# A second fold of a Fourier transform over the rows, in a hybrid encoder layer

## The chip, the cores and the metric

The kernel runs on one core of one Trainium2 chip. The metric is the device time of one execution in microseconds, taken as the median of the runs. A profile of one execution gives each engine's instructions in order of time.

## The reference

Two sequences (prompt and sample) of 1024 rows and 1024 columns go through one encoder layer. Both are normalised and projected; one half of the projection feeds a latent attention with 4 heads, the other half, 512 wide in 8 groups of 64, a Fourier mixing. The results are joined, projected, added to the input, and followed by a SwiGLU feed-forward part.

```python
def fourier_group(f_in, w_four):
    b, s, _ = f_in.shape
    f = f_in.reshape(b, s, F_GROUPS, F_GROUP_DIM).astype(jnp.float32)
    fr = jnp.real(jnp.fft.fft2(f, axes=(1, 3), norm='ortho')).astype(f_in.dtype)
    out = jnp.einsum('bsgc,gcd->bsgd', fr, w_four)
    return out.reshape(b, s, FOURIER_WIDTH)

def layer(x, c, ...):
    ...
    h = rmsnorm(x, g_mix) * (1.0 + sc1) + sh1
    z = h @ w_in
    ...
    y_mla = mla_group(q_lat, kv_lat, k_pe, g_q_lat, w_uq, g_kv_lat, w_ukv)
    y_four = fourier_group(f_in, w_four)
    mix = jnp.concatenate([y_mla, y_four], axis=-1) @ w_out
    x = x + ga1 * mix
    ...
    ffn = (jax.nn.silu(h2 @ w_gate) * (h2 @ w_up)) @ w_down
    return x + ga2 * ffn
```

The real part of the 2-D transform is a cosine transform over the rows of a cosine transform over the 64 channels, less a sine transform over the rows of a sine transform over the channels. What this document is about is the transform over the 1024 rows.

## The kernel before

All products are in float32 split into a rounded high part and a low rest, so one product of the algebra is three on TensorE: `mm3` (lines 77 to 80) issues high x high, high x low and low x high, on lines 78, 79 and 80. `split` (lines 61 to 63) makes the two parts: ScalarE copies the high part, VectorE subtracts it for the low part. Nearly every line of the trace therefore carries one of these five numbers, and a reader goes by the names of the tiles.

The rows of a sequence are loaded in an order of their own, `_slots`: 512 rows t (first the even, then the odd), then for each of them its mirror 1024 - t. A first fold is in `evenodd`: the sum and the difference of a row and its mirror. So the transform over the rows needs cosines on 512 sums and sines on 512 differences.

The first stage takes pairs of 128-row blocks: `pairs` holds 2 sequences s by 4 blocks j. `fourier_in(k, i)` projects the sums (i = 0, into `zc[s]`, 280 wide: 256 cosine columns and 24 for the Nyquist channel) and the differences (i = 1, into `zs[s]`, 256 wide). Each result is one PSUM bank, copied out by ScalarE on line 450. Row 512, whose mirror is itself, and row 0 need care: row 512 is carried in `zo`, and the first block has a second version with that row replaced (`zod`, `zno`). The tables of cosines and sines come through a ring of eight buffers named `raw` (`raw_tile`, lines 602 to 615), which later also carries `wraw`, `gar` and `wor`; they are split into `tb[0]` and `tb[1]`.

The second stage begins at line 724. `zsplit(s)` splits `zc` and `zs` into `zh`; `nyq_split` does so for the Nyquist columns, `zn`. `dft(s)` multiplies them with the tables: for each column block q, four row blocks give the even outputs (258 wide, bank `pe`) and four the odd ones (256 wide, bank `po`), and then two sine blocks of four products 512 wide (`pb`). The results are split into `A`, `B` and, for the Nyquist block of both sequences together (q = 2, done in `dft(0)`), `ny`. `prep_wm(s)` loads the folded output weights `wm_d` through `wraw` and splits them into `wm`, and `wn_d` through `wnr` into `wn`; each `wnr` is first zeroed by POOL. `fourier_out(s, abn, j)` multiplies both and stores 128-row blocks of `fo_d`, through ScalarE (`ea`) and VectorE (`ed`). Beside it run `mod2` (modulation products, line 914, with 1 MB loads `wada`), and for s = 1 the loads of the attention stage: `gate_wo` loads `gar` and `wor` and lets POOL multiply them into `wog_d`, then `stage3_loads` issues `lat`, `ql`, `wqr`, `rc`, `rs` and `ckv`. The queries' rotary part, `rope_q`, reads `wq` (split from `wqr`) and stands between the row blocks of `fourier_out(1)`.

The order of each engine's instructions is written by a scheduler at build time, from the program's dependencies and from explicit wishes: `issue_after` and `behind()` put an instruction behind others on its queue, `first(early, late)` puts one ahead of another. SP issues nearly all DMAs, in its order; an issue also waits for the eighth DMA before it. Banks are eight; a pool's tile is freed when its last reader is done.

## Time and profile before

| what | value |
|---|---|
| median of 3 runs | 2072.19 us (2071.8 to 2073.34) |
| the profiled execution: span | 2070.4 us |
| TensorE busy | 98% |
| VectorE, ScalarE, POOL busy | 68%, 44%, 40% |
| granted TensorE clock, mean | 0.996 |
| DMA | 375.49 MB, mean 181 GB/s |

The page gives the profiled execution's time as its span, from the first to the last instruction. In the rows that follow, a row of an order of time has the start in microseconds, the duration, the engine, the line, the operation, the tile written and the tiles read, and in brackets the idle time ahead of it with what ended that. SPq is the DMA queue of SP; "x5" merges five equal neighbours. A row of a table by stage has busy time and number of instructions for each engine, the granted clock, the mean busy share of the 16 DMA engines and what they moved.

### The profile page before, as it was taken

The page shows a single profiled execution, that of the slowest core. Times are in us where ns is not written, and L with a number is a line of the kernel's source. Part 1 is how long each engine was busy: PE and PEld are TensorE (multiplying, and loading weights), DVE is VectorE, ACT ScalarE, POOL GpSimd, SP SyncE. Part 2 cuts the span into 40 slices and gives each one's busy share as a digit, 9 for nine tenths or more (in the row PEclk, how much of TensorE's full clock was granted, in tenths as well). Part 3 has the DMA queues.
Part 4 walks back from the last instruction along what each step waited for, and adds up shares of the span by engine and source line. Part 5 has one row for each costly group of instructions (what it writes and reads, how often), then busy time and mean ns, then how long its engine had stood idle before and what let it go on. Part 6 is the DMA issues. An engine that isn't in the chain of part 4 may idle for free.

```text
span 2070.4 us, 28813 instructions
## 1 busy us (share of the span) xinstructions
PE 2027.1 (98%) x10044; PEld 1662.3 (80%) x10044; DVE 1407.7 (68%) x2085; ACT 901.9 (44%) x1763; POOL 819.2 (40%) x1013
## 2 busy tenths in 40 slices
PE   7899999999999999999999999999999999999998
PEld 4788878888888877888888888877788888888876
DVE  4567757666676679767777676678666665667685
ACT  3666535555565564323332355454233323236441
POOL 0555211111313327779778510334554454420142
PEclk9999999999999999999999999999999999999999
DMA  9675895544644375545546487675322222258672
GB/s 389 217 244 174 265 335 184 125 90 94 168 110 133 135 259 188 199 151 200 184 153 212 165 280 256 215 233 181 118 98 102 99 106 102 88 172 277 228 230 94
DMA packets 185342, 375.49 MB, mean 181 GB/s; under 512 B 18764, under 2 KB 58444, under 8 KB 182124
## 3 DMA queue, kind: packets, MB, share of 16 engines
q1 hardware_dynamic: 167212, 318.06, 45.8%
q0 software_dynamic: 17984, 55.59, 9.0%
q8 instruction: 79, 1.29, 0.3%
q14 instruction: 67, 0.55, 0.1%
HBM read 259.47 MB, written 122.49 MB: 184 GB/s over the span
## 4 chain that ended last, share of the span: by engine, by line
PE 56%; DVE 3%; DMA 2%; issue 1%; POOL 1%; ACT 1%; SPq 0%; DVEq 0%; ACTq 0%; POOLq 0%
PE bank L80 19%; PE bank L78 19%; PE bank L79 19%; DVE wl L63 1%; DVE val L137 1%; DVE val L1590 0%; DMA draw<-s_d 0%; ACT wh L62 0%; DVE val L134 0%; DMA X<-hc_d 0%; DMA rgu<-in_wgu_dram 0%; POOL rs_y L104 0%; DMA val<-x_d 0%; DMA draw<-in_w_down_dram 0%; DMA draw<-t_d 0%
## 5 line engine op out<-in xcount | busy, mean ns | idle before, releaser
L78 PE MATMUL bank<-H,wh 128*128 128x512 f32 x1232 | 487.6, 396 | 2.1 <-DVE val L137 0.9
L80 PE MATMUL bank<-H,wl 128*128 128x512 f32 x1232 | 488.5, 397 | 0.2 <-DVE wl L63 0.2
L79 PE MATMUL bank<-H,wh 128*128 128x512 f32 x1232 | 484.5, 393 | 0.3 <-DVE H L63 0.3
L78 PEld LDWEIGHTS bank<-H,wh 128*128 128x128 f32 x1232 | 231.2, 188 | 58.7 <-DVE val L137 1.8
L79 PEld LDWEIGHTS bank<-H,wh 128*128 128x128 f32 x1232 | 231.3, 188 | 58.0 <-DVE H L63 0.6
L80 PEld LDWEIGHTS bank<-H,wl 128*128 128x128 f32 x1232 | 231.2, 188 | 56.8 <-DVE wl L63 0.5
L63 DVE TENSOR_TENSOR wl<-draw,wh 128x512 fp32r<-128x512 f32 x286 | 201.4, 738 | 89.7 <-ACT wh L62 89.3
L137 DVE TENSOR_TENSOR val<-bank,val 128x512 f32<-128x512 f32 x200 | 136.6, 689 | 159.4 <-PE bank L80 156.0
L62 ACT CAST wh<-draw 128x512 fp32r<-128x512 f32 x286 | 168.8, 619 | 162.1 <-PE bank L79 82.2
L137 POOL TENSOR_TENSOR val<-val 128x512 f32<-128x512 f32 x58 | 82.1, 1422 | 368.2 <-DVE val L1564 187.2
L79 PE MATMUL bank<-wl,wh 128*128 128x512 f32 x572 | 224.0, 392 | 2.7 <-DVE wl L63 2.7
L62 ACT CAST wh<-rgu 128x512 fp32r<-128x512 f32 x172 | 106.7, 621 | 269.6 <-PE bank L79 211.3
L78 PE MATMUL bank<-wh 128*128 128x512 f32 x572 | 222.8, 390 | 0.0
L80 PE MATMUL bank<-wh,wl 128*128 128x512 f32 x572 | 222.7, 389 | 0.0
L62 ACT CAST wh<-val 128x512 fp32r<-128x512 f32 x133 | 82.2, 621 | 270.4 <-PE bank L79 249.5
L63 DVE TENSOR_TENSOR wl<-val,wh 128x512 fp32r<-128x512 f32 x133 | 134.0, 1009 | 77.6 <-ACT wh L62 77.5
L63 DVE TENSOR_TENSOR wl<-rgu,wh 128x512 fp32r<-128x512 f32 x172 | 170.6, 992 | 3.6 <-ACT wh L62 3.6
L134 POOL TENSOR_TENSOR val<-rgu 128x512 f32<-128x512 f32 x80 | 118.2, 1478 | 99.2 <-DMA rgu<-in_wgu_dram 95.5
L79 PEld LDWEIGHTS bank<-wl,wh 128*128 128x128 f32 x572 | 107.3, 188 | 28.7 <-DVE wl L63 6.8
L78 PEld LDWEIGHTS bank<-wh 128*128 128x128 f32 x572 | 107.4, 188 | 23.3 <-ACT wh L62 0.8
L80 PEld LDWEIGHTS bank<-wh,wl 128*128 128x128 f32 x572 | 107.4, 188 | 22.1
L1043 DVE TENSOR_REDUCE mx<-ps_s 128x1 f32<-128x1024 f32 x64 | 78.2, 1221 | 62.2 <-PE ps_s L1038 62.0
(356 smaller groups left out, 4117.0 us busy)
## 6 DMA issues: line engine op xcount, KB each, us to landing
rgu<-in_wgu_dram SPq DMA_DIRECT2D x86, 512.0 KB, 4.2
draw<-s_d SPq DMA_DIRECT2D x143, 256.0 KB, 4.1
s_d<-val POOLq DMA_DIRECT2D x88, 256.0 KB, 4.1
draw<-t_d SPq DMA_DIRECT2D x88, 256.0 KB, 4.4
s_d<-val SPq DMA_DIRECT2D x66, 256.0 KB, 3.6
draw<-in_w_down_dram SPq DMA_DIRECT2D x55, 256.0 KB, 4.9
wada<-in_w_ada_dram SPq DMA_DIRECT2D x11, 1024.0 KB, 8.4
xt<-in_x_dram SPq DMA_DIRECT2D x16, 512.0 KB, 10.0
```

The lines of the kernel that those rows point to most:

```text
L62: here["a"] = nc.scalar.copy(hi, src).ins
L63: here["v"] = nc.vector.tensor_tensor(out=lo, in0=src, in1=rd(hi), op=ALU.subtract).ins
L78: nc.tensor.matmul(out, lh, rh, start=first, stop=False, skip_group_check=cont)
L79: nc.tensor.matmul(out, lh, rl, start=False, stop=False, skip_group_check=cont)
L80: here["t"] = nc.tensor.matmul(out, ll, rh, start=False, stop=last, skip_group_check=cont).ins
L134: return eng.tensor_tensor(out=out, in0=x, in1=y, op=ALU.subtract).ins
L137: eng.tensor_tensor(out=out, in0=x, in1=y, op=ALU.add)
L1043: nc.vector.tensor_reduce(out=mx, in_=ps, axis=AX.X, op=ALU.max)
```

## The change

The rows are folded a second time, around row 256: cosines of even outputs are the same for rows t and 512 - t, those of odd outputs opposite, and for the sines the other way round. `_slots` now places row t and row 512 - t in neighbouring blocks (j even, j odd). In `fourier_in` the even block is copied out by ScalarE as before; for the odd block VectorE forms the difference and then the sum of it with the even block straight from PSUM, so `zc` and `zs` hold sums and differences. `dft` then needs two row blocks for the even outputs and two for the odd ones, and for the sines two row blocks for each half of the outputs. The rows that have no partner (0, 256, 512) are put into spare rows or into a small tile `zx`, which one more table, `tcor`, brings in by two products for each column block. `zod`, `zno` and their copies go. The tables shrink to two row blocks each, `c2` and `pk` move into buffers of other tiles, and `first` names another instruction.

```diff
@@ fourier_in
-            here["z"] = nc.scalar.copy((zc, zs)[i][s][:, j, :], pc[:, : n1 - n0]).ins
+            z = (zc, zs)[i][s]
+            if j % 2 == 0:
+                nc.scalar.copy(z[:, j, :], pc[:, : n1 - n0])
+            else:
+                nc.vector.tensor_tensor(out=z[:, j, :], in0=z[:, j - 1, :], in1=pc[:, : n1 - n0], op=(ALU.subtract, ALU.add)[i])
+                here["z"] = nc.vector.tensor_tensor(out=z[:, j - 1, :], in0=z[:, j - 1, :], in1=pc[:, : n1 - n0],
+                                                    op=(ALU.add, ALU.subtract)[i]).ins
+            if j == 1:
+                if i == 0:
+                    nc.vector.tensor_copy(zx[0:1, NCOS * s : NCOS * s + NCOS], pc[0:1, :NCOS])
+                    nc.vector.tensor_copy(zx[0:1, 2 * NCOS + NNYQ * s : 2 * NCOS + NNYQ * s + NNYQ], pc[0:1, NCOS:NZC])
+                    if s == 1:
+                        nc.sync.dma_start(zc[1][0:1, 1, :], zo[2:3, :])
+                else:
+                    nc.vector.tensor_copy(zs[s][0:1, 1, :], pc[0:1, :NZS])
...
-                nc.vector.tensor_copy(zo[0], po[:ZOW, :NZC])
-                nc.sync.dma_start(zo[1], zo[0][2:3, :])
+                nc.vector.tensor_copy(zo, po[:ZOW, :NZC])
+                nc.vector.tensor_copy(zc[0][0:1, 1, :], po[0:1, :NZC])
@@ tables
         for k, n in enumerate((NT, 512)):
-            for c in range(4):
+            for c in range(2):
                 raws[k, c] = raw_tile("raw")
...
+            if k == 0:
+                raws["cor"] = raw_tile("raw")
+                nc.sync.dma_start(raws["cor"][:, :NTE], a["tcor"])
...
+            nc.scalar.copy(tcor, raws["cor"][:, :NTE])
@@ nyq_split, zsplit
-            for i in range(2):
-                nc.vector.tensor_copy(zno[i], rd(zn[i][:, 0, :]))
-            for s in range(2):
-                ss = slice(NNYQ * s, NNYQ * s + NNYQ)
-                split(zno[0][0:1, ss], zno[1][0:1, ss], zo[s][0:1, NCOS:])
+            split(zxs[0], zxs[1], zx)
...
-                            first(here["a"], here["z"])
+                            first(here["v"], here["z"])
                             first(here["v"], here["ny"])
-                if k == 0:
-                    for i in range(2):
-                        nc.vector.tensor_copy(od[i], rd(z[0][i][:, 0, :]))
-                    split(od[0][0:1, :], od[1][0:1, :], zo[s][0:1, :NCOS])
@@ dft
-                for c in range(4):
-                    zz = [(zn[i] if q == 2 else z[0][i][:, :, sl])[:, c, :] for i in range(2)]
-                    mm3(pe[:m, :NTE], zz[0], zz[1], tb[0][0][:, c, :NTE], tb[0][1][:, c, :NTE], c == 0, c == 3)
-                for c in range(4):
...
-                    mm3(po[:m, :256], zz[0], zz[1], tb[0][0][:, c, NTE:NT], tb[0][1][:, c, NTE:NT], c == 0, c == 3)
+                for c in range(2):
+                    mm3(pe[:m, :NTE], zz[0][:, 2 * c, :], zz[1][:, 2 * c, :], tb[0][0][:, c, :NTE], tb[0][1][:, c, :NTE], c == 0, False)
+                for i in range(2):
+                    nc.tensor.matmul(pe[:m, :NTE], zxs[i][:, x0 : x0 + m], tcor, start=False, stop=i == 1)
+                for c in range(2):
+                    mm3(po[:m, :256], zz[0][:, 2 * c + 1, :], zz[1][:, 2 * c + 1, :],
+                        tb[0][0][:, c, NTE:NT], tb[0][1][:, c, NTE:NT], c == 0, c == 1)
...
-                for c in range(4):
-                    mm3(pb, z[1][0][:, c, sl], z[1][1][:, c, sl], tb[1][0][:, c, :], tb[1][1][:, c, :], c == 0, c == 3)
+                for v in range(2):
+                    ks = slice(256 * v, 256 * v + 256)
+                    for c in range(2):
+                        mm3(pb[:, ks], z[1][0][:, 2 * c + v, sl], z[1][1][:, 2 * c + v, sl],
+                            tb[1][0][:, c, ks], tb[1][1][:, c, ks], c == 0, c == 1)
@@ _slots
-    t = np.concatenate([np.arange(0, 512, 2), np.arange(1, 512, 2)])
+    ev, od = np.arange(0, 256, 2), np.arange(1, 256, 2)
+    t = np.concatenate([ev, [256], 512 - ev[1:], od, 512 - od])
```

More of the change, by code (lines that the diff above doesn't have):

```diff
@@ L49 @@
 NT = 514
+NX = 2 * (NCOS + NNYQ)
 @with_exitstack
@@ L156, in hybrid_encoder_kernel @@
     zs = [zp.tile([P, 4, NZS], F32, name=f"zs{s}") for s in range(2)]
-    zo = [zp.tile([ZOW, NZC], F32, name="zo"), zp.tile([1, NZC], F32, name="zo1")]
+    zo = zp.tile([ZOW, NZC], F32, name="zo")
+    zx = zp.tile([P, NX], F32, name="zx")
+    nc.gpsimd.memset(zx, 0.0)
     with ExitStack() as st:
@@ L737, in hybrid_encoder_kernel @@
         zn = [wa.tile([P, 4, NY2], F32R, name=f"zn{i}") for i in range(2)]
-        zno = [wa.tile([P, NY2], F32R, name=f"zno{i}") for i in range(2)]
+        zxs = [wa.tile([P, NX], F32R, name=f"zx{i}") for i in range(2)]
         nyt = w.tile([P, NT], F32R, name="ny")
@@ L754, in zsplit @@
                  for k in range(2)]
-            od = [wa.tile([P, NCOS], F32R, tag=f"zo{i}", name=f"zod{i}", bufs=1) for i in range(2)]
             for k, src in enumerate((zc[s], zs[s])):
@@ L799, in dft @@
                 pb = bank2()
[L800 to L801 removed]
+                for v in range(2):
+                    ks = slice(256 * v, 256 * v + 256)
+                    for c in range(2):
+                        mm3(pb[:, ks], z[1][0][:, 2 * c + v, sl], z[1][1][:, 2 * c + v, sl],
+                            tb[1][0][:, c, ks], tb[1][1][:, c, ks], c == 0, c == 1)
                 split(B[0][:, q, :], B[1][:, q, :], pb)
@@ L886, in hybrid_encoder_kernel @@
         nyq_split()
-        tb[1] = [wa.tile([P, 4, 512], F32R, name=f"tb1{i}") for i in range(2)]
+        tb[1] = [wa.tile([P, 2, 512], F32R, name=f"tb1{i}") for i in range(2)]
         with behind():
-            for c in range(4):
+            for c in range(2):
                 split(tb[1][0][:, c, :], tb[1][1][:, c, :], raws[1, c][:, :512])
@@ L1717, in _constants @@
     tsin = np.sin(2 * np.pi * ((t[:, None] * np.concatenate([ke[:256], ko])[None, :]) % N) / N)
+    tsin[0, 256:] = 2 - ko % 4
+    tcor = np.zeros((P, NTE))
+    tcor[0, :257] = -(ke % 4)
     cmask = np.zeros((P, 7))
```

28 lines of the change are left out of this document (13 added, 15 removed).

## The prediction

> **What bounds the kernel now.** I read the page's head first, then a table by stage, then the order of time on each engine around the Fourier stage.
>
> ```profile
> span 2070.4 us, 28813 instructions
> ...
> PE 2027.1 (98%) x10044; PEld 1662.3 (80%) x10044; DVE 1407.7 (68%) x2085; ACT 901.9 (44%) x1763; POOL 819.2 (40%) x1013
> ```
>
> TensorE is busy for 98% of the span, so products taken out are worth their time wherever nothing else is late. Whether something is shows only by stage:
>
> ```profile
> core 0: us, PE busy (x) PEld busy (x) DVE busy (x) ACT busy (x) POOL busy (x), PEclk, DMA share, GB/s
> 103.50:227.80 124.30, 124.02 (x791) 107.69 (x791) 81.95 (x170) 74.36 (x188) 63.64 (x142) 1.00 0.66 206
> 227.80:242.70 14.90, 14.49 (x98) 13.15 (x97) 14.21 (x37) 12.07 (x31) 0.52 (x1) 1.00 0.93 308
> 242.70:278.40 35.70, 35.70 (x183) 21.88 (x181) 19.50 (x34) 9.81 (x18) 1.34 (x2) 1.00 0.89 312
> 278.40:290.00 11.60, 11.60 (x79) 10.58 (x76) 10.46 (x21) 7.32 (x17) 0.53 (x1) 1.00 0.85 269
> 290.00:302.50 12.50, 12.35 (x56) 9.72 (x54) 5.60 (x15) 3.23 (x6) 7.60 (x9) 1.00 1.04 399
> 302.50:320.50 18.00, 18.00 (x92) 13.71 (x93) 11.16 (x23) 7.91 (x15) 8.77 (x10) 1.00 1.03 385
> ```
>
> The second row is `dft(0)`, the fourth `dft(1)`, the third and the last two `fourier_out`. In `dft(0)` VectorE is busy for 14.21 of 14.90 us, in `dft(1)` for 10.46 of 11.60. From 290 us the DMA engines are full (1.04, then 1.03). The three resources end nearly together; the change makes only one shorter.
>
> **What the products save.** TensorE in order of time:
>
> ```profile
> 228.48 0.39 PE L80 MATMUL bank<-tb,zh 128*128 128x258 f32 x1 [0.28 <-DVE zh L63]
> ...
> 237.26 0.39 PE L78 MATMUL bank<-tb,zh 128*128 128x512 f32 x1
> ...
> 242.74 0.40 PE L78 MATMUL bank<-wm,A 128*128 128x512 f32 x1
> ...
> 278.63 0.28 PE L79 MATMUL bank<-tb,zh 128*128 128x258 f32 x1
> ...
> 284.23 0.39 PE L78 MATMUL bank<-tb,zh 128*128 128x512 f32 x1
> ...
> 302.50 0.50 PE L78 MATMUL bank<-wq_h,ql 128*128 128x256 f32 x2 [0.15 <-ACT wq_h L62]
> ```
>
> From 278.63 to 284.23 stand 47 steps, 0.119 us for each product 256 or 258 wide; from 237.26 to 242.74 stand 24, 0.228 us for each 512 wide. A cosine column block goes from 24 products to 14 (6 even, 2 with `tcor`, 6 odd). There are three blocks in `dft(0)`, two in `dft(1)`: 30 and 20 products fewer, 3.6 and 2.4 us. The sine part keeps 24 products in each pass, 256 wide instead of 512: 24 x 0.109 = 2.6 us each. Together 6.2 us in `dft(0)`, 5.0 us in `dft(1)`, 11.2 us in all, 0.54% of the span.
>
> The Trainium skill ("TensorE: Matmul & The Clock Gate", section "Back-to-back issue gap") speaks against the sine half: in a stream of weight loads and matmuls the spacing is set by both, about 131 ns at 512 columns and 81 ns at 128, so the 48 narrower products would save at most 48 x 0.05 = 2.4 us instead of 5.2 (an estimate from that page). This trace does not agree: its widths are 0.228 and 0.119 us apart, almost a half.
>
> **First projection stage (to 227.8 us).** ScalarE loses eight copies out of PSUM, VectorE gains sixteen sums and differences and some one-row copies. VectorE has 124.3 - 82.0 = 42 us free there, and the added work is near 16 x 0.4 us + 8 x 0.3 us = 9 us (0.4 us from the 128x256 row below). I cost it at nothing; if that cover failed at one pair, TensorE would wait one such group, 1.5 us. The `zx` memset is ahead of anything that POOL waits for; `c2` and `pk` share buffers whose next users come long after their last reader; three table loads fewer and three `wm` loads sooner fall where the DMA share is 0.66. The new one-row DMA and the latent stores queued behind it on SP have no reader in this stage. All at nothing.
>
> **Start of dft(0).** Here the change puts work in front of TensorE.
>
> ```profile
> 227.75 1.28 DVE L63 TENSOR_TENSOR zh<-zc,zh 128x512 fp32r<-128x512 f32 x2
> 228.95 0.42 DVE L740 TENSOR_SCALAR ny<-raw 128x514 fp32r<-128x514 f32 x1
> ...
> 229.69 0.42 DVE L63 TENSOR_TENSOR zn<-zc,zn 128x96 fp32r<-128x96 f32 x2
> ...
> 231.96 2.48 DVE L63 TENSOR_TENSOR tb<-raw,tb 128x512 fp32r<-128x512 f32 x4
> ...
> 280.87 0.42 DVE L63 TENSOR_TENSOR A<-bank,A 128x256 fp32r<-128x256 f32 x1
> 281.21 0.74 DVE L818 SCALAR_TENSOR_TENSOR wn<-wnh,cmask,wnr 128x512 fp32r<-128x512 f32 x1
> ```
> ```profile
> 228.00 0.37 ACT L450 COPY zs<-bank 128x256 f32<-128x256 f32 x1 [1.21 <-PE bank L80]
> ```
>
> `first` now ties the split of `zc` to an eviction on VectorE. In the built order VectorE takes the first half of the last `zs` eviction before the two `zh` splits. It waits for the bank that ScalarE could read at 228.00, so it ends at 228.4, the splits at 229.0 and 229.6. TensorE's third product starts at 229.1, not 228.48: 0.6 us lost. Then VectorE takes the second half (0.36 in step), `ny` 0.34, two sine splits 1.2, two `zn` 0.35, and the new low part of `zx`, 560 wide, 0.7 by the 512-wide step of 0.6: to 232.6. TensorE's 12th product reads it and would be due at 230.5: 2.0 us lost. 54 products of 0.119 us remain, so `dft(0)` ends at 239.1 instead of 242.74: 3.6 us of 6.2 kept. VectorE then still has two `tb`, four `A`, two `B`, the `ny` group and eight `wm` pieces, near 10.7 us by these rows, to 243.2, while the first `fourier_out` needs the last `wm` pieces from about 242.5 on: another 0 to 1.4 us lost. Kept: 2.2 to 3.5 us; I take 2.5, since VectorE stood no moment still here before.
>
> **dft(1) and the loads behind it.** All times up to the next part are counted as if `dft(1)` still began at 278.4.
>
> ```profile
> 273.04 0.45 SPq L814 DMA_DIRECT2D wnr<-wn_d  x1
> ...
> 277.55 0.32 SPq L862 DMA_DIRECT2D fo_d<-ed  x1
> 277.92 2.40 SPq L827 DMA_DIRECT2D wraw<-wm_d  x5
> 282.56 0.32 SPq L814 DMA_DIRECT2D wnr<-wn_d  x1
> 282.92 0.43 SPq L827 DMA_DIRECT2D wraw<-wm_d  x1
> 283.40 0.92 SPq L873 DMA_DIRECT2D gar<-ga_d  x2
> 284.41 2.55 SPq L878 DMA_DIRECT2D wor<-wo_d  x4
> 287.05 1.75 SPq L703 DMA_DIRECT2D lat<-lat_d  x2
> ```
> ```profile
> 302.04 0.41 ACT L62 CAST wq_h<-wqr 128x256 fp32r<-128x256 f32 x1 [0.41 <-DMA wqr<-wq_d]
> ```
> ```profile
> wraw<-wm_d SPq DMA_DIRECT2D x16, 256.0 KB, 4.3
> wor<-wo_d SPq DMA_DIRECT2D x8, 256.0 KB, 6.3
> lat<-lat_d SPq DMA_DIRECT2D x2, 1024.0 KB, 11.1
> wog_d<-wor POOLq DMA_DIRECT2D x8, 256.0 KB, 5.6
> ...
> ql<-lat_d SPq DMA_DIRECT2D x4, 256.0 KB, 8.2
> ...
> gar<-ga_d SPq DMA_DIRECT2D x2, 256.0 KB, 6.1
> wqr<-wq_d SPq DMA_DIRECT2D x2, 256.0 KB, 10.6
> wnr<-wn_d SPq DMA_DIRECT2D x4, 96.0 KB, 3.7
> ```
>
> TensorE leaves `dft(1)` 5.0 us sooner, and its new order weaves two row blocks of `fourier_out(1)` together, so it waits little for the `wm` splits: worked through with the rows above it would reach `rope_q` 4.65 us sooner. But `rope_q` reads `wq`, whose landing already ended TensorE's 0.15 us wait at 302.50 (ScalarE waited for the DMA till 302.04). That landing is the end of a chain on SP: `wnr`, its split `wn` on VectorE (282.0), POOL's memset, the second `wnr` (282.56), the last `wraw`, `gar`, `wor`, `lat`, `ql`, `wqr`. In the new order `wnr` is not issued at 273.04 but behind the last `fo_d0` store of 277.55, at 277.9, and all `wm` loads behind it. It lands at 281.6 (3.7 us), is rounded by 282.2, and `wn` ends at 284.3: its three VectorE steps (0.74 the longest) and the `A` splits between them take about 2.1 us. That is 2.4 us later than before. `gar` starts at 285.8 instead of 283.4. From `gar` to the landed `wqr` the trace took 302.0 - 283.4 = 18.6 us, with the DMA engines full from 290. About two 256 KB loads less are still under way when `gar` starts, 0 to 1.3 us at the 399 GB/s of the fifth row; I take 0.7. So `wqr` lands at 302.0 + 2.4 - 0.7 = 303.7, and with the 2.5 us kept in `dft(0)` at 301.2, 0.8 us sooner than before; TensorE can begin 0.8 us sooner too, at 301.7. Being 2.5 + 4.65 us early, it is there at 295.4 and stands for 6.3 us. In its new order eight `wq` products come in a row with no `wm` product between them, which lets 0.5 to 1 us of ScalarE's casts show; I take 0.5, since the first two casts (0.41 and about 0.5 us) are the ones uncovered. Gain: 0.8 - 0.5 = 0.3 us. What follows keeps its length and its order.
>
> **Sum.** 11.2 us of products, less 2.6 and 1.1 us at `dft(0)`, less 0.35 in `dft(1)`, less 6.3 us before `rope_q` and 0.5 in it, leaves 0.3 us (0.05 of it is rounding); of the profiled 2070.4 us, 2070.1. The median of the runs is 1.8 us above this execution's span, so 2071.9 us. About 0.2% (4.1 us) is what a measurement of this kernel can tell from no change.
>
> **Rivals.**
>
> The loads are not the wall (0.30). For it: the DMA engines were not full between 278 and 290 (0.85, 269 GB/s), so the 18.6 us contain slack. At the 399 GB/s of that stage the 0.5 MB of `gar`, 1 MB of `wor`, 2 MB of `lat`, 0.5 of `ql`, 0.1 of the first `wqr` and 0.5 MB of POOL's first `wog` stores take 11.6 us, `wqr` lands at 285.8 + 11.6 - 2.5 = 294.9, and TensorE keeps all 7.1 us: 2065.1 us. Half of that slack gives 2068. Against it: `lat` took 11.1 us to land with the engines full. The Trainium skill ("DMA: Bandwidth & Descriptors", section "Specifications") puts the fabric's ceiling at 435 GB/s; by it the 4.6 MB would take 10.6 us, and the trace's 399 GB/s at a share of 1.04 agrees that little is left above.
>
> The chain on SP slips further (slower, 0.13). `lat` stands behind the fourth `wor`, whose buffer comes free with the sixth `wm` split, which VectorE now takes behind the second `wnr`'s landing: 290.6, so `lat` goes out at 291.0 instead of 287.05. If the engines have drained by then, the 15 us from `lat` to `wqr` count from there: 306.0 - 2.5 + 0.5 = 304.0, 2.0 us later than before. It passes 0.2% when both `wnr` land 1.1 us or more later than 3.7, each shifting the rest; at 1.2 us, 2076.6 us. Against it: the `gar` and `wor` loads were still landing when `lat` was issued.
>
> The added VectorE work shows in the projection stage (0.05): 1.5 us at one or two odd pairs, 2073 to 2074 us. That the products do not go is no case: the built order holds 14 and 24 of them.
>
> **Numbers.** Forecast 0.52 at 2071.9, loads not the wall 0.30, SP slip 0.13, projection 0.05. Faster 0.30 is the first rival; same 0.55 is the forecast and 0.03 of the projection case; slower 0.15 is the slip and the other 0.02. The range 2065.0 to 2075.0 takes in the first rival's bound and the projection case and leaves out the slip. The likeliest case by itself, with 2.2 to 3.5 us kept in `dft(0)` and 0 to 1.3 us of DMA backlog: 2069.9 to 2073.
>
> **What would show it.** After: products 0.119 us apart in both parts; a wait of about 2 us for `zx` on TensorE near 230 us; `dft(0)` ended near 239; a wait for `wq` of 4 to 7 us before `rope_q`, with `gar` issued near 283. If TensorE reaches `rope_q` with no wait above 1 us, I am wrong by the first rival; if `lat` is issued after a gap in DMA traffic, by the second.

## The result: slower by 0.44%

The changed kernel takes 2082.11 us (median of 5 runs, 2081.75 to 2084.17), against 2072.19 us (5 runs, 2070.89 to 2075.99): ratio 1.0044 [1.0031, 1.0056], 9.9 us longer. The prediction had 2071.9 us, a range to 2075.0 and 0.15 for slower. It forecast a time all but unchanged, 0.3 us less; the kernel became slower, and the time lies outside the range.

The head of the page of the changed kernel:

```profile
span 2082.4 us, 28692 instructions
...
PE 2023.8 (97%) x9994; PEld 1658.4 (80%) x9994; DVE 1415.4 (68%) x2095; ACT 896.3 (43%) x1749; POOL 822.6 (40%) x1014
```

The 50 products of the cosine part are gone (10044 became 9994). Yet TensorE is busy for only 3.3 us less, not 11.2, in a span 12 us longer: the busy time also counts products that a low clock stretches. The table by stage of the changed kernel says where (start and end in us, busy time and count of each engine, granted clock, DMA share, GB/s):

```profile
core 0: us, PE busy (x) PEld busy (x) DVE busy (x) ACT busy (x) POOL busy (x), PEclk, DMA share, GB/s
208.09:211.60 3.51, 3.51 (x17) 3.49 (x18) 2.83 (x8) 3.25 (x10) 2.42 (x4) 0.51 0.16 42
234.40:247.30 12.90, 10.14 (x70) 9.36 (x69) 11.33 (x27) 9.74 (x25) 0.52 (x1) 0.87 0.78 258
247.30:283.96 36.66, 36.66 (x185) 22.08 (x183) 20.26 (x33) 8.94 (x16) 1.05 (x2) 1.00 0.81 300
283.96:290.29 6.33, 6.33 (x56) 6.33 (x53) 4.97 (x12) 4.18 (x11) 0.53 (x1) 1.00 0.91 297
290.29:303.92 13.63, 13.10 (x58) 9.87 (x56) 13.23 (x19) 5.74 (x10) 7.49 (x8) 1.00 0.89 292
303.92:311.45 7.53, 0.00 (x1) 0.00 (x0) 3.56 (x7) 0.99 (x2) 1.09 (x2) 0.72 1.05 394
311.45:317.20 5.75, 5.75 (x19) 5.08 (x20) 4.14 (x11) 3.44 (x6) 1.41 (x2) 0.50 0.96 355
```

The second row is `dft(0)`, the fourth `dft(1)`. From its first product to the one behind its last, `dft(1)` takes 6.3 us where it took 11.3: the products did go. Then there is a row in which TensorE does nothing for 7.53 us with the DMA engines full, and behind it 5.75 us at half clock. TensorE's longest waits in the changed kernel from 80 to 420 us, by what ended them (total, times, longest):

```profile
PE bank L79 <- ACT wq_h L63: 7.5, 1, 7.5
PE bank L215 <- DMA wada<-in_w_ada_dram: 3.8, 1, 3.8
PE bank L81 <- DVE hl L64: 3.1, 1, 3.1
PE bank L438 <- DVE lat L423: 2.0, 2, 1.8
PE bank L795 <- DVE zx L64: 1.9, 1, 1.9
PE bank L81 <- DVE zh L64: 0.9, 1, 0.9
```

The same list of the kernel before, from 75 to 420 us, with the rows that have a counterpart (line numbers differ by 1 to 3):

```profile
PE bank L80 <- DVE hl L63: 3.2, 1, 3.2
PE bank L212 <- DMA wada<-in_w_ada_dram: 2.2, 1, 2.2
...
PE bank L80 <- DVE zh L63: 0.3, 1, 0.3
PE bank L435 <- DVE lat L420: 0.2, 1, 0.2
PE bank L78 <- ACT wq_h L62: 0.2, 1, 0.2
```

The wait for `hl` stayed; those for `wada`, `lat`, `zh` and `wq` grew, the last from 0.2 to 7.5 us, and the one for `zx` is new. From the order of time on TensorE in both, this is how far the changed kernel lags at each point, and what the part in between added:

| point | lag, us | added |
|---|---|---|
| first product of `dft(0)` (227.80, 234.57) | 6.77 | +6.8 |
| end of `dft(0)` | 4.56 | -2.2 |
| first product of `dft(1)` (278.40, 283.96) | 5.56 | +1.0 |
| end of `dft(1)` | 0.59 | -5.0 |
| ready for `rope_q` (302.35, 303.92) | 1.57 | +1.0 |
| first product of `rope_q` | 8.95 | +7.4 |
| first product of the attention stage, `ps_s` (320.72, 332.40) | 11.68 | +2.7 |
| last product | 12.0 | +0.3 |

### The profile page after: what moved, and what is told of

The parts are those of the page before. It is cut to its first block, busy times and chain, and to the rows that moved or that the text cites. A ratio compares the mean times of both kernels' runs of the same rounds, so it can differ in the third digit from the quotient of the medians.

```text
span 2082.4 us, 28692 instructions
## 1 busy us (share of the span) xinstructions
PE 2023.8 (97%) x9994; PEld 1658.4 (80%) x9994; DVE 1415.4 (68%) x2095; ACT 896.3 (43%) x1749; POOL 822.6 (40%) x1014
## 4 chain that ended last, share of the span: by engine, by line
PE 53%; DVE 3%; DMA 3%; POOL 1%; issue 1%; ACT 1%; SPq 0%; DVEq 0%; ACTq 0%; POOLq 0%
PE bank L81 18%; PE bank L80 18%; PE bank L79 17%; DVE wl L64 1%; DVE val L138 1%; DMA draw<-t_d 1%; DMA val<-x_d 1%; POOL val L138 1%; DMA draw<-s_d 1%; DMA draw<-in_w_down_dram 0%; ACT wh L63 0%; DVE val L1606 0%; DVE val L135 0%; DMA X<-hc_d 0%; DMA ga<-ga_d 0%
```

## The experiments

The theory that came out of the two traces: between `dft(0)` and the attention stage the time is set by loads, stores and buffers, so TensorE's saved products become waits, and each wait costs more than its length because the granted clock falls near it; the sums on VectorE add a wait of their own in the projection stage. Its rivals: the order of the loads alone is at fault and can be mended; or the fold on VectorE alone costs it all.

Each time is a median, each ratio is to the kernel before on the same chip with its 95% interval. For reading them together, the points of TensorE's order of time in each trace (us; `rope_q` and `ps_s` by the start of their first product, the other two by the end of the last product; the last column is the ratio, from all runs and not from the trace alone):

| kernel | end of `dft(1)` | `rope_q` | first `ps_s` | last product | ratio |
|---|---|---|---|---|---|
| before | 289.9 | 302.5 | 320.7 | 2060.8 | 1 |
| after | 290.5 | 311.5 | 332.4 | 2072.8 | 1.0044 |
| e1 | 288.5 | 304.9 | 329.4 | 2075.9 | 1.0058 |
| e7 | 291.8 | 304.2 | 324.9 | 2069.5 | 1.0034 |
| e8 | 289.0 | 308.9 | 330.6 | 2072.7 | 1.0045 |
| e9 | 285.4 | 297.8 | 323.9 | 2068.9 | 1.0032 |
| e11 | 287.2 | 300.3 | 323.6 | 2069.7 | 1.0023 |
| b4 | 283.8 | 304.3 | 325.6 | 2067.5 | 1.0025 |
| m1 | 290.4 | 305.1 | 325.6 | 2067.1 | 1.0038 |
| m2 | 290.9 | 303.2 | 321.3 | 2061.1 | 1.0013 |
| m3 | 284.8 | 297.1 | 316.0 | 2055.8 | 1.0012 |
| v0 | 289.1 | 301.4 | 319.5 | 2067.8 | 1.0037 |
| v1 | 287.8 | 300.1 | 319.1 | 2065.5 | 1.0024 |

### The order of the loads

**`wqr` ahead of `lat`.** In `stage3_loads`:

```diff
-        for i in range(2):
-            then(rd(lat[i]), lat_d[0][i][:, 2:4, :])
         wqr = [...]
         ...
         then(rs, a["ropes"])
+        for i in range(2):
+            then(rd(lat[i]), lat_d[0][i][:, 2:4, :])
```

> The changed kernel with one order altered: of the attention stage's loads, `ql` and `wqr` go out ahead of the two 1 MB `lat` loads. Theory (the wait is the load order): the first `wqr` no longer counts 15.0 us from the issue of `lat` (296.01 to 311.00 in the changed kernel), but stands behind 2.7 MB of `gar`, `wor`, `wog` and `ql`; it lands near 302 to 304, where TensorE arrives at 303.9. The wait of 7.5 us falls under 1 us, the low granted clock behind it goes with it, and the time is 2072 to 2074 us. Rival 1 (the DMA engines are full, so the order matters little): the landing moves by 2 to 3 us at most, the wait stays at 4 to 5 us, 2079 us. Rival 2 (the lateness only moves on): `lat` then lands 5 us later and the first products of the attention stage wait for it instead, 2081 to 2083 us.

Measured: 2086.2 us, 1.0058 [1.0043, 1.0073]. TensorE's waits in its trace:

```profile
PE ps_s L1050 <- DVE ed L138: 5.3, 1, 5.3
...
PE bank L80 <- DVE wm L848: 2.7, 1, 2.7
```

The 7.5 us for `wq` are gone, and 5.3 us stand at the first `ps_s` instead. The lateness moved on to the next thing that needs a load or a freed buffer; the time did not fall. Behind the first `ps_s`, too, this trace is slower: to the last product it takes 1746.5 us, where the kernel before takes 1740.1 and the changed one 1740.4.

**`wm(1)` loaded early.** The loads of `wnr` and `wraw` for s = 1 are taken out of `prep_wm(1)` and issued beside the last `wada`, alone (e6) and with the order of e1 (e7):

```diff
                     mod2(2 * n)
+                    if n == 2:
+                        load_wm(1)
                     mod2(2 * n + 1)
```

> The changed kernel with the ten loads of `wm` and `wn` for s = 1 issued in the third row block of `fourier_out(0)`, behind the last `wada` load, instead of behind the last `fo_d0` store (`wnr` gets a second buffer for it). Theory (the wait for `wq` is set by when the block of loads starts): 2.1 MB move from 284 to 273 us, where the DMA share has room (0.81 from 248 to 284); `gar` no longer waits for the second `wnr`, `lat` goes out at 291 instead of 296, `wqr` lands near 306, the wait of 7.5 us shrinks to 2 to 3 us: 5 us sooner than the changed kernel, a ratio of 1.002 to before. Rival (the DMA engines have no room there either): `mod2` waits for its last `wada` loads by as much, ratio 1.004.

> Both orders: the `wm` loads for s = 1 early and `ql` and `wqr` ahead of `lat`. The run with `wqr` ahead alone lost its wait for `wq` and stood 5.3 us at the first product of the attention stage, with the DMA engines full until then. Theory (the amount of loads up to the attention stage is the wall, and 2.1 MB of it now go earlier): that wait falls under 1 us too, ratio 1.000 to 1.002. Rival (the wall is in the order on SP, not the amount): still 4 to 5 us there, ratio 1.005.

Measured: e6 2085.98 us, 1.0049 [1.0033, 1.0065]; e7 2081.3 us, 1.0034 [1.0022, 1.0046]. In e6 `gar` goes out at 283.96 instead of 291.01 us, but `lat` only at 292.33 and TensorE still waits 7.3 us for `wq`: `wqr` followed `lat`, not `gar`. (This trace is of the fastest of e6's four runs, 2080.9 us; the others are 2085.9 us and more.) In e7 that wait is gone, and 2.6 and 1.2 us stand at `ps_s`.

**The low part of `zx` first.** `dft(0)`'s two waits are shortened: the split of `zx` ahead of those of `zn`, `zsplit`'s sine half behind `nyq_split`, and the difference tied by `first` instead of the sum:

```diff
-        zsplit(0)
-        nyq_split()
+        zsplit(0)                 # calls nyq_split between its two halves
@@ nyq_split
+            split(zxs[0], zxs[1], zx)
             for s in range(2):
                 ...
-            split(zxs[0], zxs[1], zx)
```

> The changed kernel with VectorE's order at the start of dft(0) altered: the two `zh` splits ahead of both halves of the last `zs` eviction, and `zx` and `zn` ahead of the sine splits. The waits of 0.9 us for `zh` and 1.9 us for `zx` in dft(0) go. Theory (what dft(0) gives is taken back behind it, where loads set the times): `mod2` or `rope_q` stand as much longer, and the ratio to before stays at 1.0035 to 1.0045. Rival (the loads follow TensorE, as their buffers come free with its products): all that follows is 2.8 us sooner, ratio 1.003.

Measured: 2084.16 us, 1.0045 [1.003, 1.006]. `dft(0)` takes 9.9 us instead of 12.9, 3.0 less, and the time is that of the changed kernel (1.0044). In the trace the gain goes bit by bit: two waits for `wm` (2.2 us in all), a wait for `wq` that is still 5.6 us; TensorE is 2.6 us ahead of the changed kernel at `rope_q`, 1.8 at the first `ps_s`, and level at the last product (2072.72 against 2072.80). So a shorter `dft(0)` does not shorten the whole, as its theory had it. Single traces of one kernel differ by some 5 us at the end, though, so this trace alone does not show where each part went.

**All of these together,** with the one-row copies on ScalarE (e9); with the second four `wor` loads moved from behind the first row block of `fourier_out(1)` to behind its last as well (e10); with ten buffers in the ring as well (e11):

```diff
-                    nc.vector.tensor_copy(zs[s][0:1, 1, :], pc[0:1, :NZS])
+                    nc.scalar.copy(zs[s][0:1, 1, :], pc[0:1, :NZS])
@@ e10
-                if (s, j) == (1, 1):
+                if (s, j) == (1, 0):
                     gate_wo(1, None, here["st"])
@@ e11
-tag="raw", name=name, bufs=8)
+tag="raw", name=name, bufs=10)
```

> All orders together: `wm` loads for s = 1 early, `ql` and `wqr` ahead of `lat`, the order of the `zx_first` run in dft(0), and the one-row copies of the fold by ScalarE instead of VectorE. Theory: the waits for `wq`, `zh` and `zx` are gone, the one in the projection stage is 0.9 us shorter, the loads end 5 us earlier; ratio 0.998 to 1.000, so the halved products pay at last. Rival (a wall of loads that no order of issue removes): ratio 1.001 to 1.003.

> The run with all orders, and besides the second four `wor` loads (`gate_wo(1)`) moved from behind the first row block of `fourier_out(1)` to behind its last, so that the `fo_d1` stores no longer queue behind them on SP. With all orders TensorE stood 6.6 us before the attention's first product, then ran 4 us at low clock. Theory (that wait is the queue on SP: stores, `ed` buffers and banks behind `wor`): the wait falls under 2 us, the low clock goes, 6 us sooner: ratio 0.999 to 1.001. Rival (the DMA engines are full up to there, whatever stands first): the wait stays over 4 us or comes back as a wait for `wvr` in the attention stage; ratio 1.002 to 1.004.

> As the run with `wor` late, and ten instead of eight buffers in the ring `raw`, so that `gar` doesn't wait for two `wm` splits of VectorE. Theory: `gar` goes out 5 us sooner (at 281 instead of 286), the DMA share from 280 to 290 us rises from 0.67 to 0.9, and what waits for loads behind it is 2 to 3 us sooner: ratio 0.998 to 1.000. Rival (there is no wait left that these loads end): as the run without.

Measured: e9 2081.45 us, 1.0032 [1.002, 1.0044]; e10 2080.64 us, 1.0039 [1.0026, 1.0053]; e11 2078.13 us, 1.0023 [1.0013, 1.0034]. In e9 TensorE comes to the attention stage at 317.3 us, 3.4 us ahead of the kernel before, and then:

```profile
PE ps_s L1072 <- ACT ed L897: 6.6, 1, 6.6
```

In e7, e9, e10 and e11 TensorE was ready for this product between 317 and 324 us, and it started at 324.9, 323.9, 323.7 and 323.6. The order and the buffers are worth up to 0.2% (e11 against the changed kernel), and a wall stands behind it that none of these moved. Nor is this wall all: from the first `ps_s` to the last product e7, e9 and e11 take 4.5 to 6.0 us more than the kernel before. In e9 2.1 us of this lie in the first hundred products, where the clock is low behind the wait; the rest is not explained.

### The fold on VectorE

**Plain copies in place of the sums and differences** (the products over half the rows stay; their inputs are not folded), alone (e3) and with the order of e1 (e5):

```diff
-            if j % 2 == 0:
-                nc.scalar.copy(z[:, j, :], pc[:, : n1 - n0])
-            else: ...
+            here["z"] = nc.scalar.copy(z[:, j, :], pc[:, : n1 - n0]).ins
```

> The changed kernel without the fold: in the odd blocks too ScalarE copies the bank out, as before the change, and the sums, differences and one-row copies of VectorE are left out, so the products take unfolded rows. Theory (VectorE's added work is what makes the projection stage longer): the 1.8 us wait for `lat` at 206 us and the low clock behind it (1.4 us) go, dft(0) begins 3 to 4 us sooner, near 231, the 0.9 us wait for `zh` goes, and everything behind keeps this: 2078 us. Rival (the stage is longer for other reasons: where the small tables lie, the order of loads): the wait at 206 us stays, 2081 to 2083 us.

> Both of these: the fold left out (products take unfolded rows) and `ql` and `wqr` ahead of `lat`. It is the halved products without the work that makes them possible. Theory (the products are worth their 11.2 us where nothing else stands in front of TensorE): no wait for `wq` over 1 us, 2072.2 - 11.2 + about 2.3 us of other loss in the projection stage + 1.9 us for `zx` = 2065 us. Rival (the loads bound this stretch whatever their order): 2072 us or more.

Measured: e3 2079.48 us, 1.0026 [1.0015, 1.0037]; e5 2085.13 us, 1.0053 [1.0038, 1.0068]. Without the fold TensorE's waits for `zh` and `zx` are gone, and the one for `lat` near 206 us is 0.25 us in e3 but still 1.2 us in e5. In e5 5.1 us stand at the first `ps_s`, as in e1. The same place in the changed kernel, in order of time on VectorE, POOL and TensorE (start, duration; in brackets the idle time and its cause):

```profile
196.19 0.41 DVE L462 COPY zx<-bank 1x256 f32<-1x256 f32 x1
...
199.47 0.40 DVE L458 TENSOR_TENSOR zs<-zs,bank 128x256 f32<-128x256 f32 x1
...
200.13 1.27 DVE L64 TENSOR_TENSOR eol<-eo,eoh 128x512 fp32r<-128x512 f32 x2
...
201.49 2.54 POOL L397 TENSOR_TENSOR eo<-hf 128x512 f32<-128x512 f32 x2 [5.03 <-DVE eol L64]
...
207.55 0.48 DVE L423 TENSOR_SCALAR lat<-bank,rs_r 128x256 f32<-128x256 f32 x1 [1.78 <-POOL rs_r L109]
...
208.09 1.06 PE L438 MATMUL bank<-ident,lat 128*128 128x128 f32 x4 [1.82 <-DVE lat L423]
```

The fold stands on VectorE ahead of the split `eol`; POOL waits 5.03 us for `eol` before it may overwrite `eo`, `lat` comes behind, and TensorE stands. 7.4 us lie between `eol` and `lat` here as in the kernel before (194.23 and 201.65): what moved is `eol`. The fold is not the whole of the loss, in this stage either. From the first transposes of `lat` (93.0 us in the kernel before, 95.5 in the changed one) to the first product of `dft(0)` it took 134.8 us in the kernel before and 135.0 in its repeat, 139.0 and 140.4 in the changed one and its repeat, but also 136.6 in e3 and 137.6 in e5: about half of the lengthening stays without the fold, and no run says why. And e3 is still slower than the kernel before, with a wait of 4.3 us for `wq`.

### How much is to be moved

**The kernel before with half its products.** No fold, no other change; two of the four row blocks are left out of the products:

```diff
-                for c in range(4):
+                for c in range(2):
                     zz = ...
-... c == 0, c == 3)
+... c == 0, c == 1)
```

> The kernel before, with half of the transform's products over the rows left out (two of the four row blocks everywhere in dft(s)) and nothing else changed: no fold, no work on VectorE, no extra table. TensorE loses 60 products 256 to 258 wide and 24 of 512, 60 x 0.119 + 24 x 0.228 = 12.6 us. Theory (from dft(0) to the attention stage the loads set the time: 30.8 MB in 92.9 us at a DMA share of 0.94): most of it turns into waits for `wq` and at the attention's first product, with low clock behind them; ratio 0.997 to 1.000. Rival (the loads follow TensorE, and the change loses its gain only by the work that it adds): ratio 0.994 to 0.995, 11 to 12 us.

Measured: 2078.82 us, 1.0025 [1.0015, 1.0034]. Taking products out of the kernel before and adding nothing makes it slower: 12.6 us of them by the prediction's spacings, and the two `dft` became 10.7 us shorter (15.1 and 11.5 us became 8.9 and 7.0). Its waits, two stretches of its table by stage, and its queue on SP:

```profile
PE bank L78 <- ACT wq_h L62: 4.2, 1, 4.2
...
PE bank L78 <- ACT wm L831: 2.1, 2, 1.8
PE bank L79 <- DVE wm L63: 2.0, 1, 2.0
PE bank L78 <- ACT zod L62: 0.8, 1, 0.8
```
```profile
286.30:289.70 3.40, 3.21 (x8) 2.53 (x9) 3.40 (x7) 2.27 (x4) 0.12 (x1) 0.56 0.60 135
300.00:310.00 10.00, 5.79 (x20) 4.82 (x20) 6.91 (x17) 4.53 (x8) 1.87 (x4) 0.69 1.05 405
```
```profile
270.42 6.41 SPq L862 DMA_DIRECT2D fo_d<-ed  x4
276.93 0.61 SPq L814 DMA_DIRECT2D wnr<-wn_d  x1
...
286.87 0.84 SPq L873 DMA_DIRECT2D gar<-ga_d  x2
```

9.1 us of waits took the place of the products, with the DMA engines full from 300 to 310 us, and half clock behind them. So the sign does not need what the change adds. The size, 0.25%, is that of e3. But b4 is not the kernel before with fewer products and nothing else: the build orders the instructions anew. Its first `wnr` stands behind all four stores of `fo_d` and goes out at 276.93 instead of 273.04, its first `gar` at 286.87 instead of 283.40, although TensorE is ahead; the changed kernel has the same order. How much of the 0.25% is this order and how much is TensorE's being early, b4 does not separate. The order alone is not the cause: e9 and e11 send `gar` out at 280.9 and 280.1, ahead of the kernel before, and are slower all the same.

**Less to move.** The gating of the output projection for sequence 0 (its reads of `wor`, POOL's products and the stores of `wog_d`, 4.2 MB) is left out: of the changed kernel (m1), of the one before (m2), of e9 (m3).

```diff
-            for h in range(HEADS):
-                r = raw_tile("wor")[:, :512]
-                ...
-                    nc.gpsimd.dma_start(wog_d[:, h, gs], r)
```

> The changed kernel without the gating of the output weights for the first sequence: the eight `wor` loads, POOL's products and the eight `wog_d` stores are left out (4.2 MB, ten microseconds of full DMA engines, of the 30.8 MB between dft(0) and the attention stage), and `wvr` takes the ungated weights. Theory (the loads hold this stretch): the chain to `wqr` loses its four `wor`, the wait for `wq` shrinks from 7.5 to 2 to 4 us, nothing is stretched on VectorE by POOL; ratio 1.001 to 1.002. Rival (TensorE's waits come from the order of issue, not from the amount): the wait stays over 6 us, ratio 1.004.

> The kernel before with the same 4.2 MB left out. Both theories: TensorE waits for loads nowhere in this stretch (0.2 us), so it gains 0 to 1 us: ratio 0.9995 to 1.000. It is the base for the other two.

> The run with all orders, and the same 4.2 MB left out. With all orders TensorE came to the attention stage 3.8 us ahead of the kernel before and stood there 6.6 us. Theory (that wall is the amount of loads and stores): it stands under 1 us, no low clock follows, and the halved products pay: ratio 0.997 to 0.998. Rival (a wall that is not the amount): still 4 to 6 us of wait, ratio 1.002 to 1.003.

Measured: m1 2081.13 us, 1.0038 [1.0025, 1.0051]; m2 2076.51 us, 1.0013 [1.0003, 1.0022]; m3 2077.05 us, 1.0012 [0.9999, 1.0025]. The waits do go: for `wq` 1.1 us in m1 instead of 7.5, and in m3

```profile
PE ps_s L1064 <- ACT ed L897: 0.7, 1, 0.7
```

instead of 6.6. In m3's trace TensorE is at the attention stage 4.7 us ahead of the kernel before, and its last product ends 5.0 us ahead. So the wall of e9 was this gating: its traffic, its buffers or POOL's products beside VectorE, which m3 takes out together.

The times of these kernels hold something else, though. In the traces of m1, m2, m3, and of v0 and v1 below, which have no `wog_d` stores either, 13.3 us lie between TensorE's last product and the end of the span; in each of the other 15 traces it is 9.6. The last work on VectorE in the kernel before (span 2070.4 us) and in m2, under the span of its trace:

```profile
2065.53 0.88 DVE L1671 TENSOR_SCALAR val<-val,rs_r 128x512 f32<-128x512 f32 x2 [1.80 <-POOL rs_r L108]
```
```profile
core 0 of [0], span 2074.4 us
2065.89 0.88 DVE L1663 TENSOR_SCALAR val<-val,rs_r 128x512 f32<-128x512 f32 x2 [1.81 <-POOL rs_r L108]
```

The work ends 0.4 us later in m2, the span 4.0 us later. Why the close of these programs takes 3.7 us (0.18%) more is not known; it lies behind the last work of every engine. Taken off, as an estimate from the traces, m1 stands at 1.0020, where its theory had it, and m2 and m3 at 0.9995 and 0.9994, level with the kernel before. By this estimate leaving out the gating changes nothing for the kernel before and brings the changed one nearer to it. Between m2 and m3, which close alike, the halved products with their orders gain nothing in the median (2076.51 and 2077.05 us), against 5.4 us by their traces; but m3's trace is of the fastest of its ten runs, which lie between 2070.8 us (mean granted clock 0.996) and 2083.7 us (0.992).

**The same work later.** The gating of sequence 0 is moved into the attention stage, on the form that sequence 1 has there: for the kernel before (v0) and for e9 (v1).

```diff
-        last = gate_wo(0, gate_after, None)
+        last = here["wraw"]
...
+            todo[0].append(lambda g=g: gate_half(0, g))
             todo[0].append(lambda g=g: wv_load(0, g))
```

> The kernel before with the same move of the gating and nothing else: the base for the version with all orders. Theory: nothing in the stretch waited for these loads, ratio 0.999 to 1.001, and the version with all orders is faster than this one by 0 to 4 us. Rival (the move of the gating is itself a gain, and what the other version gains is its work): ratio under 0.998.

> The version with all orders, in which the output weights of the first sequence are gated in the attention stage, as those of the second sequence are (POOL multiplies `wvr` there), so that `gar`, `wor` and `wog_d` leave the stretch without anything being left out of the result: 4.7 MB less. Theory (amount and order of loads hid the gain of the halved products): TensorE comes to the attention stage 4 to 5 us ahead of the kernel before and stands under 1 us; ratio 0.998 to 1.001, by how often the granted clock falls. Rival (POOL's eight products of 1.3 us now stand before the first `wv` splits): new waits in the attention stage, ratio 1.002 or more.

Measured: v0 2081.34 us, 1.0037 [1.0025, 1.005]; v1 2078.45 us, 1.0024 [1.0014, 1.0034]. On this base, which closes alike, the halved products with their orders are 2.9 us faster than without (nine runs of 2077.4 to 2080.6 us against five of 2080.1 to 2082.8): the one pair in which they pay, by about a quarter of their 11.2 us. The move itself costs the kernel before 0.37%. Half of that is the longer close, without which v1 would stand at 1.0006; in v0's trace the first hundred products of the attention stage take 23.6 us instead of 18.5, with a wait of 2.6 us for `nb`. No version that was run beat the kernel before.

### The clock

**Products that keep TensorE busy.** 24 products into a spare bank ahead of `rope_q`, nothing else:

```diff
+                    idle = bank2()
+                    for n in range(24):
+                        nc.tensor.matmul(idle, abn[0][0][:, 0, :P], abn[1][0][:, 0, :], start=n == 0, stop=n == 23)
                     for u in range(2):
                         rope_q(0, 0, u, bank2)
```

> The changed kernel with 24 more products, 512 wide, put into the wait for `wq` before `rope_q`; they read operands that are there and their result is read by nobody: 24 x 0.235 = 5.6 us inside the wait of 7.5 us. Theory (the granted clock falls because TensorE stood idle): the landing of `wqr` stays at 311.0, the clock stays at 1.00 in the 6 us behind it, so the 256-wide products of `rope_q` stand 0.119 apart and not 0.215, the 512-wide ones 0.235 and not 0.43: 2.5 us sooner, 2079.5 us. Rival (the fall of the clock has a cause of its own, such as a limit over a longer time): it stays, 2082 us, or moves to another place.

Measured: 2082.05 us, 1.0039 [1.0024, 1.0054], the changed kernel's time. The clock stayed at full rate behind them; but `wq` was cast by 312.4 us and the products ran to 314.6, so 2.2 us of what they saved was lost again. TensorE also came to them only at 309.1 us, behind a new wait of 2.7 us for `wm` with half clock behind it, where it stood ready at 303.9 in the changed kernel. That no fall follows when TensorE stays busy is seen in this one trace; what that is worth could not be told.

**Each kernel again,** unchanged, for the scatter of a trace:

> The changed kernel once more, beside the others on one chip. Theory: ratio 1.0044 within 0.0012; the projection stage ends 4 to 7 us later than the 227.8 us of the kernel before, by where the falls of the clock lie, of which 1.8 to 2.6 us is the wait for `lat` near 206 us in every trace; the wait for `wq` is 6 to 8 us.

> The kernel before once more, for a second trace of it. Theory (the granted clock falls for about 3.3 us after some of TensorE's waits, and at which of them is a matter of phase): the projection stage ends within 2 us of 227.8, by where the falls lie, and no wait over 0.3 us stands between 92 and 340 us.

Measured: after 2081.31 us, 1.0043 [1.0026, 1.0059], with waits of 4.1 (`wada`), 2.9 (`lat`), 5.8 (`wq`) and 1.9 us (`zx`); before one run, 2077.3 us, whose trace starts `dft(0)` 1.1 us and ends 5.1 us later than the first. Both expectations missed in part: the projection stage of the changed kernel ended 9.3 us later than 227.8, its wait for `wq` is under 6 us, and the kernel before has a wait of 0.8 us for `B`. The waits of the changed kernel come again in their places, with other sizes; single traces of one kernel differ by some 5 us at the end.

The falls can be counted over all runs without a trace, by the mean granted clock: 0.9953 over 79 runs of the kernel before, 0.9923 over 9 runs of the changed one. The missing share of the span is 9.8 and 16.0 us. By this reckoning up to 6 of the 9.9 us are low clock; b4 stands at 0.9929, 14.8 us. It is an upper figure: the mean also counts low clock while TensorE stands still, as in the row of 7.53 us at 0.72, which costs nothing.

## Why the prediction was wrong

**The products: right.** In the changed kernel

```profile
284.18 0.28 PE L80 MATMUL bank<-tb,zh 128*128 128x258 f32 x1
...
290.17 0.28 PE L81 MATMUL bank<-tb,zh 128*128 128x256 f32 x1
```

are 50 steps apart: 0.120 us each, for the sine products too. `dft(1)` lost 4.97 us (predicted 5.0). The 131 and 81 ns of the Trainium skill ("TensorE: Matmul & The Clock Gate", section "Back-to-back issue gap") were rightly put aside for this kernel.

**The start of `dft(0)`: right in mechanism, near in size.** TensorE's two waits in order of time:

```profile
235.85 0.39 PE L81 MATMUL bank<-tb,zh 128*128 128x258 f32 x1 [0.88 <-DVE zh L64]
...
239.31 0.58 PE L795 MATMUL bank<-tcor,zx 128*128 128x258 f32 x1 [1.88 <-DVE zx L64]
```

0.88 and 1.88 us (predicted 0.6 and 2.0); about 1.3 us of low clock behind the second, from 239.3 to 242.3 us, were not in the sum, and no `wm` piece was late. Kept: 2.2 us, predicted 2.5.

**The projection stage: the first step that failed.** "I cost it at nothing" rested on 42 us in which VectorE is idle over the whole stage. The wait of 1.8 us in this trace (2.9 in its repeat) is longer than the bound of 1.5 us, and it counts in full. With the 3.51 us at a clock of 0.51 behind it (1.7 us lost) that is 3.5 of the 6.8 us by which `dft(0)` starts late; 0.8 us stay unplaced. The other 2.5 us were there at the first transposes of `lat` (95.5 us against 93.0), ahead of the fold's first sum at 102.4: a wait for `wada` of 3.8 us instead of 2.2, and a clock of 0.60 behind it:

```profile
87.99:92.25 4.26, 4.26 (x16) 2.94 (x17) 2.15 (x5) 2.46 (x6) 2.83 (x8) 0.60 1.00 391
```

In the kernel before the clock fell earlier, between the waits for `hl` and `wada`, so that its 1.6 us came out of the second wait:

```profile
79.70:83.00 3.30, 3.30 (x11) 2.90 (x10) 2.82 (x5) 0.00 (x0) 0.40 (x1) 0.51 0.69 195
```

Both ways occur among the changed kernels (after, its repeat, e8 and e10 wait about 4 us for `wada`; the others 2.0 to 2.4), so I do not count this part as the change's.

**The chain on SP: right up to `gar`, wrong behind it, as the second rival had it.** SP's queue in the changed kernel:

```profile
282.81 0.32 SPq L878 DMA_DIRECT2D fo_d<-ed  x1
283.23 0.38 SPq L830 DMA_DIRECT2D wnr<-wn_d  x1
283.65 3.27 SPq L843 DMA_DIRECT2D wraw<-wm_d  x7
290.12 0.32 SPq L830 DMA_DIRECT2D wnr<-wn_d  x1
290.48 0.42 SPq L843 DMA_DIRECT2D wraw<-wm_d  x1
291.01 0.84 SPq L889 DMA_DIRECT2D gar<-ga_d  x2
293.07 2.85 SPq L894 DMA_DIRECT2D wor<-wo_d  x4
296.01 0.86 SPq L725 DMA_DIRECT2D lat<-lat_d  x2
```
```profile
311.00 0.40 ACT L63 CAST wq_h<-wqr 128x256 fp32r<-128x256 f32 x1 [5.23 <-DMA wqr<-wq_d]
```

`dft(1)` began 5.56 us later than the 278.4 of the prediction; with that shift, `gar` was due at 291.4 and went out at 291.01. `lat` was due at 291.0 + 5.56 = 296.6 by the rival and went out at 296.01, behind the fourth `wor`; and from there the landed `wqr` took 15.0 us, as in the kernel before (287.05 to 302.04). So the forecast's term of 0.7 us for two loads less was wrong and the rival's "the 15 us from `lat` to `wqr` count from there" right: `wqr` was due at 303.7 + 5.56 = 309.3 and landed at 311.0, 1.7 us later. The rival got 0.13 because "the `gar` and `wor` loads were still landing": they were, and it made no difference to these 15 us. The first rival, that the loads are not the wall, fell: the wait was 7.5 us.

**The price of a wait: the second step that failed.** The sum took TensorE's 6.3 us ahead of `rope_q` for a rest that costs nothing but its length, and said "what follows keeps its length and its order". It did not: the stretch to the attention stage took 2.7 us more, for 5.75 us at half clock. With the other falls it makes up the difference of the mean clock, up to 6 us. Saved time that turns into waits was booked at zero, and with the low clock behind the wait it came out below zero here. For the range this meant that no case of mine could pass 2076.6.

**What adds up.** By the medians, halved products cost 0.25% where nothing is added (b4, with the order that the build gives it; e3, which has them without the fold, gives 0.26%), and the fold brings the rest of the 0.44%, nearly 4 us, though the intervals of e3 and of the changed kernel overlap. By the mean clock up to 6 of the 9.9 us are low clock, shared between the two. That the saved products turn into waits for loads, with low clock behind them, is shown in the traces; what each of early arrival, order and clock costs by itself is not. Still open are the half of the longer projection stage that stays without the fold, the 1.0 us that `fourier_out(0)` took more, why a typical run of m3 is 6 us behind its traced one, and the price of one wait by itself, which e2 failed to separate.

## What to carry to other kernels

A share of 98% for the busiest engine does not say that its work is worth its time: look at the stretch, and where the DMA engines are nearly full there (0.94 over 93 us in the kernel before), take out the products alone first, without paying for it, as b4 did. If that is not faster, look for what the engine waits for before building what buys it, and compare the order of the queues too, which a build can change. When an engine comes early, follow what it will wait for next, through the load's issue, the buffer that the load needs and its place in the queue, and price the low clock near that wait too. Idle time of an engine over a stage is no cover for work put ahead of one instruction that another engine waits for. And where an experiment leaves work out, compare the end of the span as well as the stretch: five of these runs closed 3.7 us later for a reason outside it.

## What the runs showed of the hardware

**The clock falls near waits shorter than expected.** TensorE stood for 1.82 us to 208.09, and the clock was 0.51 for the next 3.5 us; 0.50 for 5.75 us after the 7.53 us; b4 has 0.56 for 3.4 us after 2.0. A like wait is not always followed by a fall: at the same place as the 1.82 us, e1 and e7 waited 2.1 and 2.2 us with none behind. The wait of 3.1 to 3.2 us for `hl` near 79 us is in every trace, and in after, its repeat, e8 and e10 the fall comes only behind the next wait. The Trainium skill ("TensorE: Matmul & The Clock Gate", section "Part 1: The HAM clock gate", "What's actually happening") tells of a half rate set by activity in a free-running window of about 3.4 us; the falls of 3.3 to 3.5 us here and their wandering place agree. Its section "HAM oscillation" gives idle gaps above about 3.4 us as what to avoid; here the clock fell behind a wait of 1.8 us.

**POOL's products stretch VectorE's.** In e2, VectorE and POOL in order of time:

```profile
299.24 3.69 DVE L848 SCALAR_TENSOR_TENSOR wm<-wraw,cmask,wm 128x512 fp32r<-128x512 f32 x1
...
299.88 2.49 POOL L896 TENSOR_TENSOR wor<-wor,gar 128x512 f32<-128x512 f32 x2
```

The step on VectorE takes 0.74 us in the kernel before (each of its eight); beside two products of POOL it took 3.69, and TensorE waited 2.7 us for it, and so in e1 (3.70 and 2.7). The Trainium skill ("GPSIMD Engine Reference", section "1. Specifications") says that the two share interfaces to SBUF and contend when VectorE reads two operands there, which this step does. Moving loads moves this clash as well.

**`wqr` lands 12 to 15 us behind `lat`, wherever `gar` stands.** From the issue of `lat` to the landed `wqr` it took 15.0 us in the kernel before, in the changed one and in e6, and 12.0 to 14.9 in e2, e3, e8, b4, m1 and the repeat of the changed kernel, though `gar` went out from 0.9 us (m1, without `wor` between) to 8.4 us (e6) ahead of `lat`. Where `lat` stood behind it, in e9, `wqr` took 4.7 us from its own issue. The prediction counted from `gar`, the wrong end.
